# q and k transposed whole and split behind the transpose; scores as three 32-row products; interleaved tap chains

## The chip, the cores and the metric

The kernel runs on one core of a Trainium2 chip. The metric is the time of one execution on the device in microseconds (us); lower is better. The engines are called as the profile calls them: PE (TensorE; its weight loads are shown apart as PEld), DVE (VectorE), ACT (ScalarE), POOL (GpSimd) and SP, whose queue issues most DMAs.

## The reference

Two layers of a decoder trunk on 512 tokens of width 1024, in f32. The part that the change touches, cut to what matters:

```python
u = rmsnorm(h, mix_norm[i]) @ w_in[i]                 # 9 blocks of 256 columns
a_val, a_gate, pool_in, q, k, v, gb, gc, sv = split(u)
# conformer mixer: a causal depthwise convolution of 31 taps, then layer norm and silu
y = causal_dwconv(a_val * sigmoid(a_gate), conv_w) + conv_b
# differential attention: 4 heads, each with 2 q/k pairs of 32 dims, v of 64 dims
q, k = apply_rope(q), apply_rope(k)
sc = einsum("bqhcd,bkhcd->bhcqk", q, k) * 32 ** -0.5
a = softmax(where(causal, sc, -inf)); a = a[:, :, 0] - lam * a[:, :, 1]
o = rmsnorm(a @ v, subln_g) * (1 - lam_init)
h = h + concat([y_a, y_b, y_c, y_d]) @ w_out[i]
h = h + hier_moe(rmsnorm(h, ffn_norm[i]), ...)        # 16 experts, two per token
h = h + sigmoid(rmsnorm(h, ple_norm[i]) @ ple_gate_w[i] + b) * (p[i] @ ple_proj[i])
```

## The kernel before, in words

The 512 tokens are four tiles of 128. Each layer goes through five stages in order: `project` (the input projection and three of the mixers), `attend` (attention, the output projection, norms and router logits), `route`, `experts` and `combine`. Every engine takes its instructions in the order in which the program issues them, and that order is written by hand.

Products that must keep f32 accuracy are done in fp32r, a form that PE streams in one pass: each operand is split into a rounded high part and a remainder, and three products are added, high by high, high by low and low by high (`mm3`, lines 255 to 257). ACT makes the high part and DVE the remainder, for weights at L228 and L239.

`attend` is a loop of 18 ticks. Tick n starts the scores of step n (query tile n // 4, head n % 4), takes the maxima of step n - 1 (L770, DVE), its exponentials (L784, ACT) and the combination of the two softmaxes (L797, DVE), transposes the result of step n - 2 (L804, PE, evicted at L806 by ACT) and multiplies that of step n - 3 by v (L816, PE). The list `TICK` is the order within a tick, and `FILL1` and `FILL2` say how many half products of the output projection (`wo_mm`, added into h at L750 by DVE) PE does in between. What is left of the 31 taps of each half of the convolution channels waits in a queue from which `due` takes a few in each tick, as `TAPS` tells (L483, DVE), then the layer norm of that mixer. `rotate` (L632 to L635, DVE) applies the rotary tables to eight heads-and-parts of q or k of one tile.

q and k go into the scores as stacks. For a tile i and p = 0 (q) or 1 (k), `stack` lets ACT write the high part twice into `qks` (L708 the rounding, L709 the second copy) and `stack_lo` lets DVE write the remainder (L713), so that a head's 32 dims become 96: for q high, remainder, high and for k high, high, remainder. `qkt` transposes four such stacks at a time (L721, PE, 128x96 each) and evicts them (L723, ACT) into `QT` or `KT`, 96 partitions deep. One matmul of 96 rows (L762) is then the whole three-part product of one q/k pair, and a second adds the causal mask in bf16 (L763). A step has two pairs. A tile needs 4 passes of ACT of 128x256 for the stacks, 16 transposes and 4 evictions of 96x512.

Of the kernel before, what the change touches and what calls it, by code (L numbers as in the profile page):

```python
# [11 lines left out]
F32 = mybir.dt.float32  # L12
F32R = mybir.dt.float32r
# [10 lines left out]
S = 512  # L24
# [25 lines left out]
TAILU, POST, FIRST, FIRST4 = 9, 3, 5, 1  # L50
HI = {5: 1, 6: 2, 9: 3, 10: 4}

TICK = "qkt max add av out exp f1 stl turn stk due lo rot score hi f2 comb".split()
TAPS = [1.8, 2.4, 2.4, 4.8, 1.8, 1.2, 5.4, 0, 0, 0.6, 3.6, 0, 0, 1.2, 3.4, 0, 1.0, 3.4]
ROT = {0: [(2, 0)], 2: [(2, 1)], 3: [(3, 1)], 4: [(3, 0)]}
STK = {0: [(1, 1)], 2: [(2, 0)], 3: [(2, 1)], 5: [(3, 0)], 7: [(3, 1)]}
STL = {1: [(1, 1)], 3: [(2, 0)], 5: [(2, 1)], 6: [(3, 0)], 8: [(3, 1)]}
OUTD = [1, 2, 3, 4]
LND, LNT = [1, 2, 3, 4, 4, 6], [0, 1, 2, 4]
FND = [1, 1, 2, 2, 4]  # L60
# [107 lines left out]
class _Kernel:  # L168
# [262 lines left out]
    def project(self):  # L431
        nc, V, G, T, SC, w, tk = self.nc, self.V, self.G, self.T, self.SC, self.w, self.ticks
# [44 lines left out]
        def tap(m, k):  # L477
            def f():
                if k == 0:
                    V.tensor_scalar(acc[:, m], glu[:, m, 0:S], self.cwh[:, m, 0:1], self.cb[:, m:m + 1],  # L480
                                    op0=ALU.mult, op1=ALU.add)
                else:
                    V.scalar_tensor_tensor(acc[:, m], glu[:, m, k:k + S], self.cwh[:, m, k:k + 1], acc[:, m],  # L483
                                           op0=ALU.mult, op1=ALU.add)
            return f

        def ev_a():
            for m in range(2):
                V.scalar_tensor_tensor(glu[:, m, 30:], th[m], 1.0, oa[m], op0=ALU.add, op1=ALU.mult)
            for m in range(2):  # L490
                for k in range(31):
                    tk.queue.append((0.6, tap(m, k)))
            tk.queue.append((10.0, self.layer_norm))


        up = pb_.tile([128, 2, 16 + S], F32, name="up", tag="pad", bufs=1)
        G.memset(up[:, :, :16], 0.0)
        o_up = self.cm_unit(ev_a, 1.2)
        W_ = 16 + S
        sums = []  # L500
# [192 lines left out]
    def attend(self):  # L693
        V, T, SC, w, tk, sm, l = self.V, self.T, self.SC, self.w, self.ticks, self.sm, self.l
        mhi, mlo, h = self.mhi, self.mlo, self.h
        kp = self.pool("kp", side=self.side[0])
        KT = kp.tile([96, 8, S], F32R, name="KT")
        xp = self.xp
        a2 = self.pool("a2", side=self.side[1])
        QT = {}  # L700
        stk = {}


        qks = xp.tile([128, 2, 8, 3, 32], F32, name="qks", bufs=1)

        def stack(i, p):
            s_ = stk[i, p] = qks[:, p]
            SC.copy(s_[:, :, 0, :].bitcast(F32R), self.qr[i][:, 8 * p:8 * p + 8])  # L708
            SC.copy(s_[:, :, 2 - p, :], s_[:, :, 0, :])  # L709

        def stack_lo(i, p):
            s_ = stk[i, p]
            V.tensor_sub(s_[:, :, 1 + p, :].bitcast(F32R), self.qr[i][:, 8 * p:8 * p + 8], s_[:, :, 0, :])  # L713

        def qkt(i, p, b):
            s_ = stk[i, p]
            if p == 0 and b == 0:
                QT[i] = kp.tile([96, 8, 128], F32R, name="QT", bufs=2)
            pt = self.tr([128, 4, 128])
            for c in range(4):  # L720
                T.transpose(pt[:96, c], s_[:, 4 * b + c].rearrange("p a d -> p (a d)"), self.ident)  # L721
            hs = slice(4 * b, 4 * b + 4)
            SC.copy(QT[i][:, hs] if p == 0 else KT[:, hs, i * 128:(i + 1) * 128], pt[:96])  # L723

        CH = [[2, 3, 6, 7], [0, 1, 4, 5]]
        wo = {}
# [2 lines left out]
        def wo_get(kh, nh):  # L729
            wo[kh, nh] = [tuple(t.rearrange("p (c n) -> p c n", c=2) for t in w.get(0)) for _ in range(2)]  # L730
# [21 lines left out]
        st = {}  # L752

        def scores(n):
            qi, hd = divmod(n, 4)
            k = max(256, (qi + 1) * 128)
            qs_ = slice(qi * 128, (qi + 1) * 128)
            st[n] = []
            for c in range(2):
                pt = self.mm([128, 512])  # L760
                keys = KT[:, 2 * hd + c, :k] if qi else KT[:, 2 * hd + c, None, :128].to_broadcast([96, 2, 128])
                T.matmul(pt[:, :k], QT[qi][:, 2 * hd + c], keys, start=True, stop=False)  # L762
                T.matmul(pt[:, qs_], self.identb, self.maskb, start=False, stop=True)  # L763
                st[n].append(pt)

        def maxi(n):
            k = (n // 4 + 1) * 128
# [43 lines left out]
        def av(n):  # L811
            qi, hd = divmod(n, 4)
            at = st.pop(n)
            hs = slice(hd * 64, (hd + 1) * 64)
            for b in range(qi + 1):
                T.matmul(oacc[:, qi % 2, hs], at[:, b], self.vt[b][:, hs], start=(b == 0), stop=(b == qi))  # L816
# [40 lines left out]
        rr, xts, tp = {}, {}, None  # L857
# [4 lines left out]

        def fn2(i):

            p, tag = ((self.gpool, "gv0"), (xp, "qks"), (tp, "xn"), (xp, "xt"))[i]
            xx = self.scaled(i, rr[i], gffn, p, 1, "xn", tag)
            SC.dma_start(xnd[i * 128:(i + 1) * 128, :], xx)

# [26 lines left out]
        def filler(n, k):  # L895

            while k > 0 and (cur or (fill and fill[0][0] <= n)):
                if not cur:
                    a = fill.pop(0)[1]
                    cur.append((a, wo_mm(*a)))  # L900
                    next(cur[0][1])
                else:
                    (i, nh, kh), g = cur.pop()
                    next(g)
                    if (nh, kh) == (1, 1) and i < 2:
                        for d, f in zip(FND, (fn1, fn3, fn2, fn4, fn5)):
                            tk.later(d, lambda f=f, i=i: f(i))
                k -= 1

        w.limit = self.moe_start[l] + 3  # L910
        for p in range(2):
            stack(0, p)
            stack_lo(0, p)
        wo_get(0, 0)
        for p in range(2):
            for b in range(2):
                qkt(0, p, b)
        filler(0, 2)
        for p in range(2):
            self.rotate(1, p)  # L920
        wo_get(0, 1)
        stack(1, 0)
        stack_lo(1, 0)
        filler(0, 1)
        base = w.cur
        NS = 4 * NT
# [17 lines left out]
        def each(table, f):  # L944
            def g(n):
                for a in table.get(n, ()):
                    f(*a)
            return g

        steps = {  # L950
            "av": lambda n: n >= 3 and av(n - 3),
            "qkt": lambda n: n < NS - 4 and qkt(n // 4 + 1, n % 4 // 2, n % 2),
            "out": o_start,
            "add": lambda n: wo_add(),
            "max": lambda n: 1 <= n <= NS and maxi(n - 1),
            "exp": lambda n: 1 <= n <= NS and expo(n - 1),
            "turn": turns,
            "due": lambda n: tk.tick(TAPS[n]),
            "score": lambda n: n < NS and scores(n),
            "comb": lambda n: 1 <= n <= NS and comb(n - 1),  # L960
            "rot": each(ROT, self.rotate),
            "stk": each(STK, stack),
            "stl": each(STL, stack_lo),
            "lo": lambda n: w.make_lo(),
            "hi": lambda n: n in HI and w.make_hi(base + HI[n]),
            "f1": lambda n: filler(2 * n, FILL1[n]),
# [2 lines left out]
        for n in range(NS + 2):  # L969
            for a in TICK:  # L970
                steps[a](n)
# [605 lines left out]
```

## Time and profile before

| what | value |
|---|---|
| median of 3 runs | 927.7 us (925.6 to 927.95) |
| the profiled execution's own time | 925.41 us |
| its span, first to last instruction | 923.6 us |
| mean granted PE clock | 0.973 |
| busy in the span: PE, DVE, ACT | 858.0, 715.4, 519.1 us |
| `attend` of the two layers, roughly | 121 to 221 us and 572 to 673 us |

A time is in us from the start of the span. The profiled execution has 1.8 us outside of its span and is 2.3 us below the median of the runs. A matmul's row lasts from its start until its result is written, so that rows overlap: the distance from one start to the next is what a matmul costs in a stream. The same holds, less strongly, on DVE and ACT.

### The profile page before, as it was taken

Reading aid. Unit: us, or ns where it says so; the run is one execution under the profiler, and the core shown is the slowest. Engines: PE = TensorE matmul, PEld = TensorE weight load, DVE = VectorE, ACT = ScalarE, POOL = GpSimd, SP = SyncE. Lnnn points to the kernel's source line nnn. Section 1 sums busy time; section 2 is a strip of 40 time slices with the busy share of each in tenths; the row PEclk is TensorE's granted clock in tenths of the full one; section 3 lists DMA queues with packets and bytes.
Section 4 is the critical chain, followed back from the end, with each engine's and each line's share of the span. In section 5 each row is a group of like instructions: output and inputs, shape, how many; then the busy total and the mean of one; then the engine's idle time right before and its main releaser. Section 6 shows DMA issues by size and latency. Waiting matters only on the chain. (4 is left out here: it accounts for less than half of the span.)

```text
span 923.6 us, 12348 instructions
## 1 busy us (share of the span) xinstructions
PE 858.0 (93%) x4393; PEld 687.6 (74%) x4393; DVE 715.4 (77%) x1182; ACT 519.1 (56%) x945; POOL 151.2 (16%) x214
## 2 busy tenths in 40 slices
PE   7999988897999999979979999989979999998994
PEld 5888876685677777767878887767847777776783
DVE  4599989966788888746676998998478888885674
ACT  4322246853687878745433233487347778776453
POOL 2040001122222211101010300022131222111101
PEclk9999999998999999999999999989979999999998
DMA  9222230158799979563322223110958998882602
GB/s 354 106 92 96 98 114 1 46 193 309 270 347 363 370 271 340 227 234 146 114 92 92 92 103 112 49 46 24 373 216 307 359 370 324 317 321 91 260 24 91
DMA packets 35775, 179.02 MB, mean 194 GB/s; under 512 B 8064, under 2 KB 8320, under 8 KB 18944
## 3 DMA queue, kind: packets, MB, share of 16 engines
q1 hardware_dynamic: 23472, 148.49, 43.1%
q0 software_dynamic: 9792, 20.99, 6.2%
q10 hardware_dynamic: 2448, 8.73, 2.6%
q8 instruction: 35, 0.57, 0.2%
q14 instruction: 28, 0.23, 0.1%
HBM read 171.89 MB, written 23.07 MB: 211 GB/s over the span
## 5 line engine op out<-in xcount | busy, mean ns | idle before, releaser
L239 DVE TENSOR_TENSOR wl<-wr,wh 128x1024 fp32r<-128x1024 f32 x212 | 253.1, 1220 | 41.4 <-ACT wh L228 40.1
L228 ACT CAST wh<-wr 128x1024 fp32r<-128x1024 f32 x212 | 216.2, 1053 | 91.1 <-PE mm L256 60.9
L255 PE MATMUL mm<-wh,xTh 128*128 128x512 f32 x256 | 113.9, 445 | 1.0 <-ACT xTh L221 1.0
L483 DVE SCALAR_TENSOR_TENSOR acc<-glu,cwh,acc 128x512 f32<-128x512 f32 x120 | 100.5, 837 | 3.4
L257 PE MATMUL mm<-wh,xTl 128*128 128x512 f32 x256 | 101.2, 395 | 1.2 <-DVE xTl L222 1.2
L256 PE MATMUL mm<-wl,xTh 128*128 128x512 f32 x256 | 100.5, 392 | 0.0
L257 PE MATMUL mm<-nhi,wl 128*128 128x512 f32 (+1 forms) x224 | 77.3, 345 | 2.5 <-DVE wl L239 2.5
L255 PE MATMUL mm<-nhi,wh 128*128 128x512 f32 (+1 forms) x224 | 77.1, 344 | 0.0
L256 PE MATMUL mm<-nlo,wh 128*128 128x512 f32 (+1 forms) x224 | 77.0, 344 | 0.0
L255 PEld LDWEIGHTS mm<-wh,xTh 128*128 128x128 f32 x256 | 48.1, 188 | 16.9 <-issue 6.7
L1241 PE MATMUL mm<-wr,hT 128*128 128x512 f32 x128 | 60.2, 592 | 0.0
L1198 POOL DMA_INDIRECT xg<-xnd,ix x32 | 35.4, 1105 | 149.8 <-PE tr L251 136.8
L256 PEld LDWEIGHTS mm<-wl,xTh 128*128 128x128 f32 x256 | 48.2, 188 | 15.3 <-DVE wl L239 6.2
L257 PEld LDWEIGHTS mm<-wh,xTl 128*128 128x128 f32 x256 | 48.0, 188 | 12.9 <-DVE xTl L222 2.9
L255 PE MATMUL mm<-wh,mhi 128*128 128x512 f32 x128 | 54.0, 422 | 1.0 <-DVE h L750 1.0
L1203 POOL DMA_INDIRECT yd<-ys,ix x32 | 32.3, 1010 | 122.9 <-ACT ys L1243 107.3
L255 PE MATMUL mm<-wh,n3h 128*128 128x512 f32 x128 | 50.6, 395 | 0.0
L257 PE MATMUL mm<-wh,mlo 128*128 128x512 f32 x128 | 50.3, 393 | 0.0
L256 PE MATMUL mm<-wl,mhi 128*128 128x512 f32 x128 | 50.0, 391 | 0.0
L257 PE MATMUL mm<-wh,n3l 128*128 128x512 f32 x128 | 49.9, 390 | 0.0
L256 PE MATMUL mm<-wl,n3h 128*128 128x512 f32 x128 | 49.9, 390 | 0.0
L257 PEld LDWEIGHTS mm<-nhi,wl 128*128 128x128 f32 x224 | 42.4, 189 | 8.2 <-DVE wl L239 3.2
(236 smaller groups left out, 1861.6 us busy)
## 6 DMA issues: line engine op xcount, KB each, us to landing
wr<-wgu SPq DMA_DIRECT2D x62, 1024.0 KB, 9.1
wr<-wdn SPq DMA_DIRECT2D x30, 1024.0 KB, 10.8
wr<-win SPq DMA_DIRECT2D x13, 1024.0 KB, 6.2
wr<-wout SPq DMA_DIRECT2D x8, 1024.0 KB, 4.8
wr<-wpg SPq DMA_DIRECT2D x8, 1024.0 KB, 13.8
yt<-yd SPq DMA_DIRECT2D x12, 512.0 KB, 8.1
wr<-wqk SPq DMA_DIRECT2D x4, 1024.0 KB, 4.8
xnd<-xn ACTq DMA_DIRECT2D x8, 512.0 KB, 4.0
```

The source lines that it names most:

```text
L228: self.SC.copy(hi, src)
L239: self.V.tensor_sub(lo, src, h32)
L255: self.T.matmul(o, lh, rh, start=first, stop=False)
L256: self.T.matmul(o, lh, rl, start=False, stop=False)
L257: self.T.matmul(o, ll, rh, start=False, stop=last)
L483: V.scalar_tensor_tensor(acc[:, m], glu[:, m, k:k + S], self.cwh[:, m, k:k + 1], acc[:, m], op0=ALU.mult, op1=ALU.add)
L1198: return self.G.indirect_dma_start(out=dst, out_offset=None, in_=self.xnd[:, :], in_offset=bass.IndirectOffsetOnAxis(ap=col, axis=0), boun ...
L1203: return self.G.indirect_dma_start(out=self.yd[:, :], out_offset=bass.IndirectOffsetOnAxis(ap=col, axis=0), in_=src, in_offset=None, bound ...
L1241: self.T.matmul(o[nh], hT[:, c], wc[:, ns], start=(c == 0), stop=(c == 1))
```

## The change

`stack` and `stack_lo` go, and with them the tile `qks` and the two entries of `TICK` that call them. `qkt(i)` now transposes q and k of a tile as they are, four heads-and-parts of 32 dims at once (128x128), 4 transposes into one PSUM tile; ACT writes the rounded high parts of q and of k from there (two instructions of 128x256), and `qkl(i)` lets DVE write the two remainders, from PSUM too. It is called in one tick of four (`QKT = 2`) and no longer in each. `KT` and `QT` are 128 partitions deep and there is one of each for the high and for the low part; a pair's 32 dims lie in partitions r + 32c to r + 32c + 31, with r = 0 or 64 by the head. `scores` issues three products of 32 rows for each of the two pairs, the pairs in turn, and then the two masks. The taps of the two halves of the channels are queued in turn, and not all of one half before the other. `fn2(1)` writes to a tile of its own in the place of `qks`.

```diff
-        def stack(i, p):
-            s_ = stk[i, p] = qks[:, p]
-            SC.copy(s_[:, :, 0, :].bitcast(F32R), self.qr[i][:, 8 * p:8 * p + 8])
-            SC.copy(s_[:, :, 2 - p, :], s_[:, :, 0, :])
-        def stack_lo(i, p):
-            s_ = stk[i, p]
-            V.tensor_sub(s_[:, :, 1 + p, :].bitcast(F32R), self.qr[i][:, 8 * p:8 * p + 8], s_[:, :, 0, :])
-        def qkt(i, p, b):
-            s_ = stk[i, p]
-            if p == 0 and b == 0:
-                QT[i] = kp.tile([96, 8, 128], F32R, name="QT", bufs=2)
-            pt = self.tr([128, 4, 128])
-            for c in range(4):
-                T.transpose(pt[:96, c], s_[:, 4 * b + c].rearrange("p a d -> p (a d)"), self.ident)
-            hs = slice(4 * b, 4 * b + 4)
-            SC.copy(QT[i][:, hs] if p == 0 else KT[:, hs, i * 128:(i + 1) * 128], pt[:96])
+        def parts(i):
+            return QT[i], [t[:, :, i * 128:(i + 1) * 128] for t in KT]
+        def qkt(i):
+            QT[i] = [kp.tile([128, 2, 128], F32R, name=f"QT{a}", bufs=2) for a in "hl"]
+            pt = qkp[i] = self.tr([128, 2, 2, 128])
+            for p in range(2):
+                for m in range(2):
+                    T.transpose(pt[:, p, m], self.qr[i][:, 8 * p + 4 * m:8 * p + 4 * m + 4].rearrange("p a d -> p (a d)"),
+                                self.ident)
+                SC.copy(parts(i)[p][0], pt[:, p])
+        def qkl(i):
+            pt = qkp.pop(i)
+            for p, (hi, lo) in enumerate(parts(i)):
+                V.tensor_sub(lo, pt[:, p], hi.bitcast(F32))
...
+            m, r = hd // 2, 64 * (hd % 2)
+            pts = st[n] = [self.mm([128, 512]) for c in range(2)]
+            for j, (a, b) in enumerate(((0, 0), (1, 0), (0, 1))):
+                for c in range(2):
+                    rs = slice(r + 32 * c, r + 32 * c + 32)
+                    keys = KT[b][rs, m, :k] if qi else KT[b][rs, m, None, :128].to_broadcast([32, 2, 128])
+                    T.matmul(pts[c][:, :k], QT[qi][a][rs, m], keys, start=(j == 0), stop=False)
             for c in range(2):
-                pt = self.mm([128, 512])
-                keys = KT[:, 2 * hd + c, :k] if qi else KT[:, 2 * hd + c, None, :128].to_broadcast([96, 2, 128])
-                T.matmul(pt[:, :k], QT[qi][:, 2 * hd + c], keys, start=True, stop=False)
-                T.matmul(pt[:, qs_], self.identb, self.maskb, start=False, stop=True)
-                st[n].append(pt)
+                T.matmul(pts[c][:, qs_], self.identb, self.maskb, start=False, stop=True)
...
-            for m in range(2):
-                for k in range(31):
+            for k in range(31):
+                for m in range(2):
                     tk.queue.append((0.6, tap(m, k)))
...
-        for p in range(2):
-            stack(0, p)
-            stack_lo(0, p)
+        qkt(0)
         wo_get(0, 0)
-        for p in range(2):
-            for b in range(2):
-                qkt(0, p, b)
+        qkl(0)
         filler(0, 2)
         for p in range(2):
             self.rotate(1, p)
         wo_get(0, 1)
-        stack(1, 0)
-        stack_lo(1, 0)
         filler(0, 1)
```

## Rows read from the trace of the kernel before

**Rows 1.** The page's head and its busy times.
```profile
span 923.6 us, 12348 instructions
PE 858.0 (93%) x4393; PEld 687.6 (74%) x4393; DVE 715.4 (77%) x1182; ACT 519.1 (56%) x945; POOL 151.2 (16%) x214
```

**Rows 2.** Windows of `attend`: busy us per engine, PE clock, DMA share, GB/s.
```profile
122.00:170.00 48.00, 42.07 (x237) 33.41 (x237) 45.02 (x118) 32.25 (x94) 5.66 (x13) 0.97 0.19 72
170.00:178.00 8.00, 6.41 (x43) 5.15 (x42) 6.84 (x15) 7.94 (x21) 1.95 (x1) 0.95 0.00 1
178.00:220.00 42.00, 41.98 (x273) 36.41 (x273) 25.69 (x55) 22.27 (x53) 7.81 (x14) 1.00 0.56 217
573.50:621.50 48.00, 42.04 (x235) 33.39 (x236) 44.76 (x118) 31.75 (x92) 5.64 (x13) 0.96 0.19 72
621.50:630.00 8.50, 7.65 (x45) 6.24 (x43) 7.03 (x17) 8.36 (x23) 1.94 (x1) 0.81 0.01 2
630.00:672.00 42.00, 41.87 (x270) 36.25 (x270) 25.90 (x55) 22.22 (x54) 7.54 (x14) 1.00 0.62 238
```

**Rows 3.** Waits of DVE, 122.5 to 178 us: total, times, longest.
```profile
DVE fac L795 <- ACT e L784: 0.7, 1, 0.7
DVE wl L239 <- ACT wh L228: 0.6, 1, 0.6
DVE ss L833 <- ACT sq L824: 0.4, 1, 0.4
```

**Rows 4.** Timeline of DVE, first layer, start of `attend`.
```profile
122.07 0.42 DVE L713 TENSOR_TENSOR qks<-qr,qks 128x256 fp32r<-128x256 f32 x1 [2.38 <-ACT qks L708]
...
123.16 0.28 DVE L632 TENSOR_TENSOR rs<-qr,rope 128x128 f32<-128x128 f32 x1
...
126.31 2.36 DVE L239 TENSOR_TENSOR wl<-wr,wh 128x1024 fp32r<-128x1024 f32 x2 [0.56 <-ACT wh L228]
128.59 0.42 DVE L713 TENSOR_TENSOR qks<-qr,qks 128x256 fp32r<-128x256 f32 x1
128.93 0.68 DVE L750 TENSOR_TENSOR h<-h,mm 128x512 f32<-128x512 f32 x1
129.52 3.10 DVE L483 SCALAR_TENSOR_TENSOR acc<-glu,cwh,acc 128x512 f32<-128x512 f32 x4
```

**Rows 5.** Groups by line and shape: weight remainders; taps' min/median/max in ns.
```profile
L239 DVE TENSOR_TENSOR wl<-wr,wh 128x1024 fp32r<-128x1024 f32 x212 | 253.1, 1220 | 41.4 <-ACT wh L228 40.1
...
L483 DVE SCALAR_TENSOR_TENSOR acc<-glu,cwh,acc x120: 737/752/1831, 46.0 to 594.3; 128x512 f32<-128x512 f32 x120
```

**Rows 6.** Timeline of ACT, first layer, start of `attend`.
```profile
121.15 0.59 ACT L641 COPY qr<-mm 128x512 f32<-128x512 f32 x1 [2.18 <-PE mm L257]
...
125.21 2.02 ACT L228 CAST wh<-wr 128x1024 fp32r<-128x1024 f32 x2
```

**Rows 7.** Groups of ACT by line, 121 to 200 us.
```profile
L723 ACT CAST KT<-tr 96x512 fp32r<-96x512 f32 x8 | 4.6, 587 | 2.5 <-PE tr L721 2.5
...
L708 ACT CAST qks<-qr 128x256 fp32r<-128x256 f32 x8 | 3.3, 412 | 0.0
...
L822 ACT COPY on<-oacc 128x256 f32<-128x256 f32 x3 | 1.1, 377 | 0.0
```

**Rows 8.** Timeline of PE, first layer: transposes of stacks, a step of scores, streams.
```profile
122.64 1.93 PE L721 MATMUL tr<-con,qks 128*96 128x128 f32 x16 [1.59 <-DVE qks L713]
...
182.20 0.48 PE L762 MATMUL mm<-KT,QT 96*128 96x512 f32 x1
...
182.56 0.47 PE L762 MATMUL mm<-KT,QT 96*128 96x512 f32 x1
...
182.94 0.83 PE L816 MATMUL oacc<-v,at 128*128 128x64 f32 x6
...
183.90 0.39 PE L256 MATMUL mm<-wl,mhi 128*128 128x512 f32 x1
184.13 0.40 PE L257 MATMUL mm<-wh,mlo 128*128 128x512 f32 x1
...
188.27 1.86 PE L883 MATMUL mm<-par,xt 128*128 128x20 f32 x16
```

More of the change, by code (lines that the diff above doesn't have):

```diff
@@ L51 @@
 HI = {5: 1, 6: 2, 9: 3, 10: 4}
-TICK = "qkt max add av out exp f1 stl turn stk due lo rot score hi f2 comb".split()
+TICK = "qkt max add av out exp f1 qkl turn due lo rot score hi f2 comb".split()
 TAPS = [1.8, 2.4, 2.4, 4.8, 1.8, 1.2, 5.4, 0, 0, 0.6, 3.6, 0, 0, 1.2, 3.4, 0, 1.0, 3.4]
 ROT = {0: [(2, 0)], 2: [(2, 1)], 3: [(3, 1)], 4: [(3, 0)]}
-STK = {0: [(1, 1)], 2: [(2, 0)], 3: [(2, 1)], 5: [(3, 0)], 7: [(3, 1)]}
-STL = {1: [(1, 1)], 3: [(2, 0)], 5: [(2, 1)], 6: [(3, 0)], 8: [(3, 1)]}
+QKT = 2
 OUTD = [1, 2, 3, 4]
@@ L696, in attend @@
         kp = self.pool("kp", side=self.side[0])
-        KT = kp.tile([96, 8, S], F32R, name="KT")
+        KT = [kp.tile([128, 2, S], F32R, name=f"KT{a}") for a in "hl"]
         xp = self.xp
         a2 = self.pool("a2", side=self.side[1])
-        QT = {}
-        stk = {}
-        qks = xp.tile([128, 2, 8, 3, 32], F32, name="qks", bufs=1)
-        def stack(i, p):
-            s_ = stk[i, p] = qks[:, p]
-            SC.copy(s_[:, :, 0, :].bitcast(F32R), self.qr[i][:, 8 * p:8 * p + 8])
-            SC.copy(s_[:, :, 2 - p, :], s_[:, :, 0, :])
-        def stack_lo(i, p):
-            s_ = stk[i, p]
-            V.tensor_sub(s_[:, :, 1 + p, :].bitcast(F32R), self.qr[i][:, 8 * p:8 * p + 8], s_[:, :, 0, :])
-        def qkt(i, p, b):
-            s_ = stk[i, p]
-            if p == 0 and b == 0:
-                QT[i] = kp.tile([96, 8, 128], F32R, name="QT", bufs=2)
-            pt = self.tr([128, 4, 128])
-            for c in range(4):
-                T.transpose(pt[:96, c], s_[:, 4 * b + c].rearrange("p a d -> p (a d)"), self.ident)
-            hs = slice(4 * b, 4 * b + 4)
-            SC.copy(QT[i][:, hs] if p == 0 else KT[:, hs, i * 128:(i + 1) * 128], pt[:96])
+        QT, qkp = {}, {}
+        def parts(i):
[12 more added lines that the diff above has]
+                V.tensor_sub(lo, pt[:, p], hi.bitcast(F32))
         CH = [[2, 3, 6, 7], [0, 1, 4, 5]]
@@ L757, in scores @@
             qs_ = slice(qi * 128, (qi + 1) * 128)
-            st[n] = []
-            for c in range(2):
-                pt = self.mm([128, 512])
-                keys = KT[:, 2 * hd + c, :k] if qi else KT[:, 2 * hd + c, None, :128].to_broadcast([96, 2, 128])
-                T.matmul(pt[:, :k], QT[qi][:, 2 * hd + c], keys, start=True, stop=False)
-                T.matmul(pt[:, qs_], self.identb, self.maskb, start=False, stop=True)
-                st[n].append(pt)
+            m, r = hd // 2, 64 * (hd % 2)
[5 more added lines that the diff above has]
+                    T.matmul(pts[c][:, :k], QT[qi][a][rs, m], keys, start=(j == 0), stop=False)
+            for c in range(2):
+                T.matmul(pts[c][:, qs_], self.identb, self.maskb, start=False, stop=True)
         def maxi(n):
@@ L863, in fn2 @@
         def fn2(i):
-            p, tag = ((self.gpool, "gv0"), (xp, "qks"), (tp, "xn"), (xp, "xt"))[i]
+            p, tag = ((self.gpool, "gv0"), (xp, "xn"), (tp, "xn"), (xp, "xt"))[i]
             xx = self.scaled(i, rr[i], gffn, p, 1, "xn", tag)
@@ L951, in attend @@
             "av": lambda n: n >= 3 and av(n - 3),
-            "qkt": lambda n: n < NS - 4 and qkt(n // 4 + 1, n % 4 // 2, n % 2),
+            "qkt": lambda n: n < NS - 4 and n % 4 == QKT and qkt(n // 4 + 1),
+            "qkl": lambda n: n < NS - 4 and n % 4 == QKT and qkl(n // 4 + 1),
             "out": o_start,
@@ L961, in attend @@
             "rot": each(ROT, self.rotate),
-            "stk": each(STK, stack),
-            "stl": each(STL, stack_lo),
             "lo": lambda n: w.make_lo(),
```

## The prediction, made before the changed kernel ran

> **What bounds the kernel now.** I read the page first: PE is busy for 93% of the span, DVE for 77%, ACT for 56% [rows 1]. That average hides the stage that is changed, so I cut `attend` of both layers into three windows each. In the first 48 us of the loop DVE is the fullest engine, 45.02 of 48 us, with PE at 42.07 and ACT at 32.25; in the 8 us that follow ACT has 7.94 of 8; in the last 42 PE has 41.98, DVE 25.69 [rows 2]. The second layer repeats it. So one stage has three limits in turn, and a saving counts only on the engine whose turn it is. The waits of DVE confirm the first: in 55 us it waits for other engines in three places of any size, 0.6, 0.7 and 0.4 us [rows 3]. In its timeline it goes from one instruction to the next from 122.07 us on [rows 4]. [...]
>
> **The change on ACT.** A tile costs four evictions at 0.587 us (8 rows of KT in a layer, and as many of QT at the same length) and four passes for stacks at 0.412 (L708; L709 is alike) [rows 7]: 4.0 us. After it are two copies of 128x256 out of PSUM; the nearest row is L822, 0.377 us: 0.75 us. ACT is relieved of 3.2 us a tile, 13 us a layer. Nearly all of it lies where ACT has slack and is worth nothing there. It counts in two places, below.
>
> **The change on DVE, first window.** The remainder (L713, 128x256) is replaced by one of the same size read from PSUM; between a gain and a loss of 0.1 us I take nothing, eight for eight. What moves is the start.
>
> - Before: DVE stands idle for 2.38 us until ACT has made the first high part, and starts the rotation of tile 1 at 123.16 [rows 4]. After: ACT is free at 121.15 + 0.59 = 121.74 [rows 6], copies twice 0.37, and the second remainder can start at 122.5; PE's four transposes are done before that if their PSUM banks are free, since its last projection is over. DVE issues the next instruction some 0.34 us after a remainder (128.59 to 128.93), so the rotation starts at 122.83, 0.33 us earlier.
> - ACT's two weight casts stood at 125.21, behind stacks and evictions [rows 6]; they can now start near 122.5, so the wait of 0.56 us at L239 [rows 4] goes. Together 0.89.
> - The remainder at 128.59 leaves this place (0.34 earlier), but six must be made in the loop in place of five (0.34 later): nothing.
> - Taps: four in a row take 3.10 us [rows 4] at 0.752 each [rows 5], so they start 0.783 apart: each needs the one before, which writes the same accumulator. Two remainders of weights, which don't need each other, take 2.36 at 1.220 each: the second starts 0.08 before the first ends. Interleaved, neighbours belong to different accumulators, so I expect 0.752 - 0.08 = 0.67 from start to start, 0.11 less. Three such groups lie in the loop with three distances each: 9 x 0.11 = 1.0 us. The other 50 taps of a layer run in `project` under a PE that is full there, and I count them at nothing. If PE had slack there, they would be worth 5.5 us a layer; if the distance were not the dependence, the whole is 0.
>
> Sum of the first window: 1.9 us a layer.
>
> **Second window.** DVE waits 0.7 us for exponentials and 0.4 for squares, both from an ACT that is full [rows 2, 3]. One tile's 3.2 us off ACT covers these. 1.1 us, between 0 and, if PE's waits were all that counted, 1.6 (the two windows' idle of PE is 8.00 - 6.41 there).
>
> **PE.** Sixteen transposes take (1.93 - 0.27) / 15 = 0.11 us each [rows 8]; twelve of sixteen go, 1.3 us a tile, 5.3 us a layer. All of it lies in the first two windows, where PE is not the limit: it pays for the longer scores there and, beyond, is worth nothing. If DVE weren't in the way it would be worth those 5.3.
>
> The scores count in the third window, where the last four steps lie, 512 keys each, and PE is full. A step costs 182.94 - 182.20 = 0.74 us, its first half 182.56 - 182.20 = 0.36: 0.23 for the product (the stream distance, 184.13 - 183.90) and 0.13 for the mask and the change between number forms [rows 8]. I split that, as an estimate, into 0.05 for a mask and 0.09 for a change. After: six products, two masks, one change, 0.19 beside the products. No row of before has a 32-row product, so the price lies between two ends:
>
> - one after another, as everything in the stream goes: 6 x 0.23 + 0.19 = 1.55, 0.81 more, 3.2 us a layer;
> - the two pairs at the same time: 3 x 0.23 + 0.19 = 0.87, 0.13 more, 0.5 us a layer. Six loads don't forbid that: sixteen small matmuls with a load each start (1.86 - 0.27) / 15 = 0.11 apart [rows 8], 0.66 for six.
>
> I take the lower end. The two products of a pair use different rows of the array and different PSUM tiles, and PE takes up a matmul 0.23 us after one that lasts 0.39, so it doesn't wait for ends. It is a choice and not a reading.
>
> Between 96-row and 128-row products the trace shows no wait beyond those 0.09 us [rows 8]. [...]
>
> **SP and buffers.** `KT` and `QT` take less room, and the ring that opens when their pool closes issues its loads at the same tick. These move with the stage.
>
> **Sum.** 1.9 + 1.1 - 0.5 = 2.5 us a layer, 5 us for two. What follows each stage (routing, experts, a PE that is full) starts earlier by that. From the profiled 925.4 us that makes 920.4; as that execution lies 2.3 below the median of 927.7, I forecast 922.6 for the median. A difference of 0.3%, 2.8 us, is about what a measurement of this kernel can tell from none.
>
> **Rivals.**
>
> 1. *The products go one after another* (upper end): 3.0 - 3.2 a layer, 0.5 us slower, 928.2. For it: the stream shows nothing else. Chance 0.15.
> 2. *Each change of row group waits until the product before has ended* (the other side). Then a product costs its 0.39 us, a step 6 x 0.39 + 0.10 = 2.44, 1.7 more, 6.8 us a layer against 3.0 gained: 7.6 us slower, 935. It decides once a step costs more than 0.74 + 3.0 / 4 = 1.5 us. Against it: matmuls here start before the last one ends. Chance 0.12.
> 3. *Only going into the 32-row form and out of it drains*: twice 0.39 - 0.23 = 0.16 a step, 1.3 us a layer, 925.3. [...] Chance 0.10.
> 4. *A new wait on DVE.* `qkl` stands behind ACT's copies, these behind PE's transposes at the head of the tick; all that DVE has in the tick (taps, rotations, the combination) is queued behind it, and PE's transposes wait for the combination. If DVE comes early each time, it waits for four transposes and one copy, 3 x 0.11 + 0.38 = 0.7 us, at three ticks, 2.1 us a layer: 926.8. Against it: DVE comes late to what others give it in that window [rows 3]. Chance 0.08.
> 5. *The clock stays up.* The first two windows lost 0.03 x 48 + 0.05 x 8 = 1.8 us of full-rate PE time in the first layer and 0.04 x 48 + 0.19 x 8.5 = 3.5 in the second [rows 2]. If a PE with fewer waits keeps the upper level and all of that counts, 5.3 us more: 917.3. Against it: DVE holds PE back there all the same. Chance 0.09.
>
> **Numbers.** The forecast has 0.46, with its own range from 919.5 (PE's waits all gone) to 925 (the taps worth nothing and 0.4 a layer less elsewhere). Faster by over 0.3% are the forecast and rival 5: 0.55. Within 0.3%: rivals 3 and 4 and most of 1 (0.12): 0.30. Slower: rival 2 and the rest of 1 (0.03): 0.15. The range from 916 to 930 leaves out rival 2.
>
> **What would show it.** In the profile of the changed kernel: the first rotation of `attend` near 122.8, no wait of L239 for its cast there; taps 0.67 apart; ACT at under 7 of 8 us before the last window; pairs of score products that start within a few hundredths of a us, a step of some 0.87 us at 512 keys; PE still full to the end of the stage, which ends 2.5 us earlier in each layer. I am wrong if the products of a pair start 0.23 or more apart, if DVE shows a wait of its own at the new remainders, or if another engine holds what DVE gains before PE's window begins.

## The result and the profile after

The changed kernel takes 937.73 us in the median of 4 runs (936.38 to 940.7), the kernel before 927.02 us beside it: a ratio of 1.0121, 95% interval 1.0090 to 1.0152. It is slower by 1.2%, where 922.6 us and a gain were forecast. The profiled execution is the one of 936.38 us, 10.97 above the profiled one of before.

The line numbers of the changed kernel are one or a few lower: `mm3` is L254 to L256, the new transposes are L711, ACT's two copies L713, DVE's remainders L718, the scores L760, the masks L762.

The page, as in [rows 1]:

```profile
span 934.5 us, 12343 instructions
PE 867.2 (93%) x4425; PEld 687.5 (74%) x4425; DVE 708.0 (76%) x1182; ACT 497.5 (53%) x897; POOL 152.2 (16%) x214
```

DVE and ACT did become lighter, by 7.4 and 21.6 us. PE is busy for 9.2 us more. The windows of `attend`, as in [rows 2] (length, busy time of PE, PEld, DVE, ACT and POOL with their instructions, granted clock, DMA share, GB/s):

```profile
122.00:170.00 48.00, 40.91 (x222) 29.80 (x223) 41.47 (x111) 20.95 (x67) 5.65 (x13) 0.93 0.18 63
170.00:178.00 8.00, 7.54 (x38) 5.59 (x37) 7.05 (x19) 6.35 (x18) 1.27 (x1) 0.50 0.20 85
178.00:228.00 50.00, 49.17 (x318) 41.68 (x317) 30.66 (x64) 26.79 (x61) 8.22 (x16) 0.97 0.45 177
573.50:621.50 48.00, 40.78 (x228) 30.03 (x226) 39.94 (x106) 19.62 (x62) 4.52 (x9) 1.00 0.17 58
621.50:642.00 20.50, 19.53 (x81) 14.78 (x82) 15.62 (x41) 13.57 (x39) 3.08 (x5) 0.51 0.11 46
642.00:684.00 42.00, 41.98 (x281) 35.75 (x281) 22.73 (x45) 20.76 (x46) 5.79 (x14) 1.00 0.63 239
```

Two things are to be seen. No engine is full in the first window any more: DVE has 41.47 of 48 us and PE 40.91, so they wait for one another (the rows of waits below). And the clock column: all of 170 to 178 us is at the lower level (0.50; the clock's records of this execution hold two levels, 1.00 and 0.50), and in the second layer nearly all of 20.5 us (0.51). There PE is busy for 19.53 of 20.5 us, at half speed: it has become the limit by its clock. The clock's records give the stretches at the lower level between the start of the loop and its last four steps: before 3.4 and 6.8 us in the two layers, after 17.1 and 20.5.

The waits of PE, 122 to 178 us (who waits for whom, us in total, times, longest), then that of DVE at the new remainders, then the longest wait of PE in the same window of the kernel before:

```profile
PE tr L711 <- ACT QTh L713: 2.2, 4, 0.8
PE tr L802 <- DVE e L795: 1.7, 2, 1.2
PE mm L254 <- ACT e L782: 1.5, 1, 1.5
```

```profile
DVE QTl L718 <- ACT KTh L713: 6.6, 3, 5.1
```

```profile
PE tr L721 <- DVE qks L713: 2.0, 2, 1.6
```

Two places of PE's timeline after the change, the head of the loop and step 13, one with 512 keys:

```profile
121.06 0.38 PE L711 MATMUL tr<-con,qr 128*128 128x128 f32 x2
122.22 0.44 PE L711 MATMUL tr<-con,qr 128*128 128x128 f32 x2 [0.79 <-ACT QTh L713]
...
190.01 1.27 PE L875 MATMUL tr<-con,h 128*128 128x128 f32 x8
191.22 0.50 PE L760 MATMUL mm<-KTh,QTh 32*128 32x512 f32 x2
191.55 0.39 PE L760 MATMUL mm<-KTh,QTl 32*128 32x512 f32 x2
191.78 0.40 PE L760 MATMUL mm<-KTl,QTh 32*128 32x512 f32 x2
192.11 0.28 PE L762 MATMUL mm<-maskb,identb 128*128 128x128 bf16 x2
192.23 0.83 PE L814 MATMUL oacc<-v,at 128*128 128x64 f32 x6
```

The first line of waits is new: before, PE's transposes waited for DVE's remainders (2.0 us), now they wait for ACT. q's and k's transposes lie in one PSUM tile with ACT's copy of q issued between them, and k's two wait until that copy has been made: 1.16 us from pair to pair at the head, where four transposes in a stream cost 4 x 0.11 = 0.44 together [rows 8]. The wait is handed on to DVE. Of its 6.6 us at the new remainders 5.1 are the idle time at the head, where it stood idle for 2.38 us before [rows 4]; the other 1.5 us lie in the loop, in a place where DVE had no wait before.

The step: each x2 is a pair of products, whose starts in the trace are 3 to 4 ns apart (up to 20 in other steps), so they run at the same time. (In 4 of the 32 steps of the two layers the second product starts 0.35 to 0.46 us after the first.) But a step is not 0.87 us long: 191.22 to 192.23 is 1.01. The first pair takes 0.33 to the next, the second 0.23, the third again 0.33 to the mask. And ahead of the step the eight transposes (L875) take 1.21 us. The same place in the timeline of the kernel before has 1.03:

```profile
185.38 1.27 PE L877 MATMUL tr<-con,h 128*128 128x128 f32 x8
186.41 0.48 PE L762 MATMUL mm<-KT,QT 96*128 96x512 f32 x1
```

The 0.18 stand behind the last transpose: from its start to the first product it is 0.20 us, before it was 0.03, and alike at steps 12 and 15 (at step 14 it is 0.20 for 0.11). A step at 512 keys costs 1.01 + 0.18 in place of the 0.74 of [rows 8], 0.45 more.

DVE at the start of `attend`, as in [rows 4], and ACT, as in [rows 6]:

```profile
123.10 0.42 DVE L718 TENSOR_TENSOR QTl<-tr,QTh 128x256 fp32r<-128x256 f32 x1 [5.11 <-ACT KTh L713]
123.44 0.41 DVE L718 TENSOR_TENSOR KTl<-tr,KTh 128x256 fp32r<-128x256 f32 x1
123.77 0.28 DVE L631 TENSOR_TENSOR rs<-qr,rope 128x128 f32<-128x128 f32 x1
...
126.30 2.35 DVE L238 TENSOR_TENSOR wl<-wr,wh 128x1024 fp32r<-128x1024 f32 x2
128.57 0.68 DVE L745 TENSOR_TENSOR h<-h,mm 128x512 f32<-128x512 f32 x1
129.16 2.73 DVE L482 SCALAR_TENSOR_TENSOR acc<-glu,cwh,acc 128x512 f32<-128x512 f32 x4
```

```profile
121.79 0.38 ACT L713 CAST QTh<-tr 128x256 fp32r<-128x256 f32 x1
122.70 0.37 ACT L713 CAST KTh<-tr 128x256 fp32r<-128x256 f32 x1 [0.53 <-PE tr L711]
122.97 2.00 ACT L227 CAST wh<-wr 128x1024 fp32r<-128x1024 f32 x2
```

The rotation starts at 123.77 and not 122.83: both remainders wait for ACT's copy of k, that for k's transposes, those for the copy of q. The casts stand at 122.97, DVE's wait for them is gone, and four taps take 2.73 us in place of 3.10.

### The profile page after: what moved, and what is told of

Its sections match the earlier page's. It is cut to its first block, busy times and chain, and to the rows that moved or that the text cites. A ratio compares the mean times of both kernels' runs of the same rounds, so it can differ in the third digit from the quotient of the medians.

```text
span 934.5 us, 12343 instructions
## 1 busy us (share of the span) xinstructions
PE 867.2 (93%) x4425; PEld 687.5 (74%) x4425; DVE 708.0 (76%) x1182; ACT 497.5 (53%) x897; POOL 152.2 (16%) x214
## 5 line engine op out<-in xcount | busy, mean ns | idle before, releaser
L254 PE MATMUL mm<-wh,xTh 128*128 128x512 f32 x256 | 113.9, 445 | 1.0 <-ACT xTh L220 1.0
L256 PE MATMUL mm<-wh,xTl 128*128 128x512 f32 x256 | 101.2, 395 | 1.2 <-DVE xTl L221 1.2
L482 DVE SCALAR_TENSOR_TENSOR acc<-glu,cwh,acc 128x512 f32<-128x512 f32 x120 | 90.4, 817 | 0.1
L256 PE MATMUL mm<-nhi,wl 128*128 128x512 f32 (+1 forms) x224 | 77.3, 345 | 2.6 <-DVE wl L238 2.6
L254 PE MATMUL mm<-nhi,wh 128*128 128x512 f32 (+1 forms) x224 | 77.1, 344 | 0.0
L254 PEld LDWEIGHTS mm<-wh,xTh 128*128 128x128 f32 x256 | 48.1, 188 | 16.8 <-issue 6.7
L254 PE MATMUL mm<-wh,mhi 128*128 128x512 f32 x128 | 56.0, 437 | 3.7 <-ACT e L782 3.0
L782 ACT ACTIVATE e<-mm,mx 128x128 f32<-128x128 f32 (+3 forms) x64 | 33.0, 521 | 48.1 <-DVE mx L768 48.0
L256 PEld LDWEIGHTS mm<-wh,xTl 128*128 128x128 f32 x256 | 48.0, 188 | 13.0 <-DVE xTl L221 2.9
L256 PE MATMUL mm<-wh,mlo 128*128 128x512 f32 x128 | 51.9, 406 | 0.0
L254 PE MATMUL mm<-wh,n3h 128*128 128x512 f32 x128 | 50.5, 395 | 0.0
L256 PE MATMUL mm<-wh,n3l 128*128 128x512 f32 x128 | 49.9, 390 | 0.0
```

Of the source, the lines that this page charges most:

```text
L254: self.T.matmul(o, lh, rh, start=first, stop=False)
L256: self.T.matmul(o, ll, rh, start=False, stop=last)
L782: SC.activation(ee[:, :k], pts[c][:, :k], AF.Exp, bias=mx[:, c:c + 1], accum_out=sums[qi][:, c, hd:hd + 1])
```

## The experiments

Two theories stood first. A: PE has less to do in the first two windows, the clock falls there and PE runs late. B: the new waits and the price of the 32-row form account for the loss. To compare kernels by place, this table gives the time from the start of ACT's last copy out of `project` (L641, 121.15 in [rows 6]) to the last mask of step 4, of step 12 and of step 15 and to the last router product on PE, first and second layer, from each profiled timeline; and the stretches at the lower clock that lie between step 0 and step 15:

| kernel | step 4 | step 12 | step 15 | end | lower clock |
|---|---|---|---|---|---|
| before | 28.48, 28.47 | 61.73, 62.41 | 72.99, 73.67 | 99.90, 101.34 | 3.4; 6.8 |
| after | 29.22, 27.66 | 66.21, 67.67 | 78.69, 80.16 | 105.61, 107.09 | 17.1; 20.5 |
| e1_taps | 27.44, 27.44 | 60.70, 61.64 | 71.94, 74.49 | 98.88, 101.65 | 3.4; 6.8 |
| e2_four_first | 26.83, 26.81 | 63.17, 63.35 | 75.65, 75.82 | 102.58, 102.72 | 13.7; 13.7 |
| e6_dummy_late | 26.81, 26.82 | 60.16, 60.18 | 72.65, 72.65 | 99.58, 99.58 | none |
| e8_taps_again | 27.40, 27.40 | 61.59, 60.44 | 74.44, 71.68 | 101.74, 98.61 | 6.8; none |
| e12_few_tr | 27.19, 27.57 | 59.62, 62.50 | 70.88, 73.76 | 98.00, 100.68 | 6.8; 13.7 |

**The taps alone (e1_taps)**, on the kernel before:

```diff
-            for m in range(2):
-                for k in range(31):
+            for k in range(31):
+                for m in range(2):
```

> The kernel before with one part of the change alone: the taps of the two channel halves in turn. Theory A (the loss is PE's clock, which falls because PE has less to do while DVE holds it back) and theory B (the loss is waits: k's transposes behind ACT's copy of q, the scores' price) both expect the 1.0 us a layer that the prediction counted on DVE: 2 us faster than before, 925 us, taps 0.67 us from start to start, and a clock as before. A rival, that the tap order itself unsettles the stage, expects the same time as before or a slower one, and a longer stretch at the lower clock than the 3.4 and 6.8 us of before.

923.34 us (10 runs) beside 926.37: ratio 0.9975 (0.9948 to 1.0001). By step 4 it is 1.04 and 1.03 us ahead of before in the two layers. The taps are worth what was forecast for them in `attend`; that the whole kernel gains is not clear from these runs, whose interval touches no change.

**The four transposes ahead of both copies (e2_four_first):**

```diff
                     T.transpose(pt[:, p, m], self.qr[i][:, 8 * p + 4 * m:8 * p + 4 * m + 4].rearrange("p a d -> p (a d)"),
                                 self.ident)
+            for p in range(2):
                 SC.copy(parts(i)[p][0], pt[:, p])
```

> The changed kernel with all four transposes of a tile ahead of ACT's two copies, so that k's transposes no longer wait for the copy of q. Theory B: the wait of 0.8 us at the head and of 0.46 us three times a layer goes, and with it 2 to 2.5 us a layer: 932 to 934 us. Theory A: PE stands idle elsewhere instead, since DVE sets the pace there; the stretches at the lower clock stay (17 us in the first layer, 20 in the second): 936 to 938 us.

933.45 us (5 runs), 1.0076 (1.0042 to 1.0109), as theory B has it. The order with the wait costs 4.3 us in the medians, and all five runs (930.68 to 935.62) lie under the four of the changed kernel. Step 12 comes 3.0 and 4.3 us earlier than in the changed kernel, with shorter stretches at the lower clock, so part of this is clock. What the wait costs without the clock can be read up to step 4 of the second layer, where neither kernel has left the upper level: 27.66 to 26.81, 0.85 us.

**Unread transposes (e3_dummy)**, four in each of nine ticks of the changed kernel:

```diff
+        def idle_tr():
+            pt = self.tr([128, 4, 128])
+            for c in range(4):
+                T.transpose(pt[:, c], self.ident, self.ident)
```

> The changed kernel with four transposes of the identity matrix into a spare PSUM tile, whose result nobody reads, in each of the nine ticks of a layer that had transposes of stacks before and have none now: PE's work of before is put back, the waits stay. Theory A: the clock stays at its upper level in most of the stage, the stretches at the lower level shrink from 37 us in both layers to 10 or less, and the time falls to 928 to 931 us although PE does more. Theory B: the clock has nothing to do with it; 36 more groups of 0.44 us, hidden in PE's idle time or not: 938 to 945 us.

936.33 us (4 runs), 1.0117 (1.0073 to 1.0161), between the ranges of the two theories: not the gain of A, nor the loss of B. In the first layer the clock stayed up until the last router product, and step 12 came at 62.68 in place of 66.21; in the second, with the waits still in place, 17 us at the lower clock remained and step 15 came at 82.04 in place of 80.16.

**The pairs issued one after the other (e4_serial):** all three products of one row group, then all three of the other.

```diff
-            for j, (a, b) in enumerate(((0, 0), (1, 0), (0, 1))):
-                for c in range(2):
+            for c in range(2):
+                for j, (a, b) in enumerate(((0, 0), (1, 0), (0, 1))):
```

> The changed kernel with the three products of one pair issued before the three of the other, so that neighbours use the same row group. The prediction's choice of pairs at the same time (which the changed kernel's trace shows) expects six starts 0.23 us apart at 512 keys in place of three pairs, 0.65 us more a step there. Theory B: 3 us a layer more, 943 to 945 us. Theory A: PE is busy for longer in the stretch that loses its clock; if that holds the clock up, it gives back up to 6 us a layer, and the time is 934 to 940 us.

936.89 us (6 runs), 1.0108 (1.0073 to 1.0142), as the changed kernel. It lies in the range of theory A, but not for its reason: the order did not matter. The timeline of PE at a step shows why:

```profile
189.57 0.51 PE L760 MATMUL mm<-KTh,QTh 32*128 32x512 f32 x2
189.91 0.40 PE L760 MATMUL mm<-KTh,QTl 32*128 32x512 f32 x2
190.15 0.39 PE L760 MATMUL mm<-KTl,QTh 32*128 32x512 f32 x2
190.47 0.28 PE L762 MATMUL mm<-maskb,identb 128*128 128x128 bf16 x2
```

Issued as three and three, they still run as three pairs. That the order of issue did change is seen at the start of a step: the first weight loads of the two groups are 10 ns apart in 28 of the 32 steps, where they are 3 to 4 ns apart in the changed kernel. So PE starts the first product of the second group 0.33 us before the second product of the first group, which the program issues ahead of it: between row groups, PE doesn't keep to the order of the program. The experiment therefore says nothing of what one-after-another products would cost; it says that two row groups go on independently.

**The masks between the products (e5_mask_between)**, on e2_four_first: four changes of form in a step in place of two.

```diff
-                    T.matmul(pts[c][:, :k], QT[qi][a][rs, m], keys, start=(j == 0), stop=False)
+                    T.matmul(pts[c][:, :k], QT[qi][a][rs, m], keys, start=(j == 0), stop=(j == 2))
+                if j == 0:
+                    for c in range(2):
+                        T.matmul(pts[c][:, qs_], self.identb, self.maskb, start=False, stop=False)
-            for c in range(2):
-                T.matmul(pts[c][:, qs_], self.identb, self.maskb, start=False, stop=True)
```

> The changed kernel with the four transposes first (933.45), and the two masks of a step moved from its end to behind the first pair of products: the same eight matmuls, but four changes between 32-row and full-height work in a step and not two. Theory B (a change costs, about 0.18 us going in and 0.10 coming out): a step at 512 keys lasts 0.28 us longer, the distance from step 12 to step 15 grows from 12.47 by 3 x 0.28 = 0.8 us, and the kernel by between 2.2 us (only the eight steps under a full PE count) and 5 us: 935.7 to 938.5. Rival (a change is free, and the 32-row products themselves last longer than 0.23): the distance stays at 12.5 and the time at 933.5.

941.29 us (4 runs), 1.0162 (1.0132 to 1.0193), 7.8 above its own base and more than the 938.5 that theory B allows. Its timeline at a step with 512 keys:

```profile
190.25 0.50 PE L761 MATMUL mm<-KTh,QTh 32*128 32x512 f32 x2
190.69 0.29 PE L764 MATMUL mm<-maskb,identb 128*128 128x128 bf16 x2
190.91 0.50 PE L761 MATMUL mm<-KTh,QTl 32*128 32x512 f32 x2
191.24 0.40 PE L761 MATMUL mm<-KTl,QTh 32*128 32x512 f32 x2
191.57 0.88 PE L816 MATMUL oacc<-v,at 128*128 128x64 f32 x6
```

1.32 us in place of 1.01 for the same eight matmuls: two more changes cost 0.31, 0.28 was expected. So it is the change of form that costs, not the length of a 32-row product. The rest of the 7.8 us isn't taken apart: a stretch of 3.4 us at the lower clock fell also on the last steps of either layer, and from step 12 to step 15 it is 15.07 us in place of 12.48.

**The clock, with the waits mended (e6_dummy_late):** e2_four_first, with `idle_tr` as above in the ticks 5, 7, 8, 9 and 11.

> The changed kernel with the four transposes first (933.45), and four transposes of the identity, which nobody reads, in each of the ticks 5, 7, 8, 9 and 11 (20 x 0.11 = 2.2 us of PE work a layer, just ahead of and in the place where its clock fell for 13.7 us in each layer). Theory A (what is left of the loss beside the scores is the clock, and it falls because PE has less to do there): the stretches in attend shrink to the 3.4 and 6.8 us of before or vanish, and the time falls by 3 to 7 us, to 926 to 930. Rival (the clock falls where PE would wait anyway and costs nothing): 933 to 936, whether the stretches vanish or not.

926.27 us (10 runs) beside 925.34: ratio 1.0008 (0.9985 to 1.0031). 2.2 us of added work in a layer made the kernel 7.2 us faster by the medians, and 6.3 by the two ratios, each taken beside its own runs of before. The windows 170 to 178 and 619 to 639 us of e2_four_first and then of e6_dummy_late, with the columns of the windows above:

```profile
170.00:178.00 8.00, 8.00 (x36) 6.62 (x35) 7.57 (x19) 7.21 (x19) 1.94 (x1) 0.50 0.00 0
619.00:639.00 20.00, 19.98 (x101) 15.38 (x102) 15.71 (x41) 13.89 (x38) 3.08 (x5) 0.66 0.08 32
```

```profile
170.00:178.00 8.00, 6.84 (x45) 4.96 (x44) 7.78 (x18) 7.18 (x19) 1.94 (x1) 1.00 0.02 6
619.00:639.00 20.00, 18.83 (x129) 14.50 (x129) 17.99 (x44) 15.45 (x42) 3.06 (x5) 1.00 0.00 1
```

Clock 0.50 and PE full with 36 matmuls; clock 1.00 and PE with room left over 45. Up to step 4 the two kernels agree within 0.02 us; at step 12 the clock is worth 3.0 and 3.2 us a layer. The mean granted clock of a whole execution, which is on record for every run and not for the profiled one alone, says the same: 0.958 to 0.966 in the 5 runs of e2_four_first (0.963 in the median), 0.976 in the median of these 10. One of the 10 lies at 0.960 and takes 932.16 us, so the unread work lowers the chance of a fall and doesn't rule it out. In a stream without gaps, products of 512 columns start 0.43 us apart at a granted clock of 0.50 and 0.23 at 1.00 (changed kernel, L254 to L256, 179.34 to 180.19 and 182.71 to 183.63 us). As an estimate from these, 13.7 us under a PE that is full throughout would cost 13.7 x (1 - 0.23 / 0.43) = 6.4. The trace shows half of it, 3.0 to 3.2. PE had room in that place: from 165 to 170 us it is busy for 4.53 of 5 us even at the lower clock (e2_four_first), and at the upper one for 6.84 of 8 us from 170 to 178 (e6_dummy_late).

**Real work moved later (e7_refill):** e2_four_first, with the half projections that fill PE's gaps spread later: of sixteen, the last five lie in ticks 7, 8 and 9, where two lay in tick 7 (the expectation counts six).

```diff
-FILL1 = [0, 1, 1, 1, 1, 1, 0, 5, 1, 1, 1, 1, 1, 4, 0, 1, 0, 2, 1, 1, 0, 0, 0, 0, 0, 0, 0, 0, 0]
-FILL2 = [4, 0, 1, 0, 0, 1, 0, 4, 1, 0, 0, 1, 0, 0, 0, 1, 2, 1, 2, 1, 2, 2, 4, 2, 2, 2, 0, 0, 0]
+FILL1 = [0, 1, 1, 1, 1, 1, 0, 1, 1, 1, 1, 1, 1, 4, 0, 1, 0, 2, 1, 1, 0, 0, 0, 0, 0, 0, 0, 0, 0]
+FILL2 = [2, 0, 0, 0, 0, 1, 0, 1, 1, 1, 0, 1, 0, 0, 0, 1, 2, 1, 2, 1, 2, 2, 4, 2, 2, 2, 0, 0, 0]
```

> The changed kernel with the four transposes first (933.45), and real work in place of unread transposes: of the sixteen half projections that fill PE's gaps, seven are done later, so that the last six lie in ticks 7, 8 and 9 in place of two in tick 7 alone. Theory A: PE stays busier where the clock fell, the stretches of 13.7 us shrink, and the time falls by 3 to 7 us to 926 to 930 with no added work. Rival (they are wanted early, because PE has room there, and are in PE's way later): 935 or more.

937.36 us (4 runs), 1.0139 (1.0107 to 1.0171): a miss. The clock stayed up at 165 us, but in the first layer fell for 10.2 us at 144.5, behind the ticks from which the work was taken, for 3.4 at 178.7 and for 6.8 at 195.7, under the last steps. In the second it fell three times for 3.4 us up to step 12.

**The taps again, and with unread transposes (e8_taps_again, e9_taps_dummy).** The second is e1_taps with `idle_tr` in the ticks 7, 9 and 11.

> The kernel before with the tap chains interleaved and nothing else, once more and in more rounds, because its interval of 0.9948 to 1.0001 just touched no change. All theories: 923.5 to 924.5, 2 to 3 us under before, with an interval that ends below 1.

> The kernel before with interleaved taps (923.3 and 924.1), and four unread transposes in the ticks 7, 9 and 11: its attend still has 3 to 7 us at the lower clock in a layer. If that costs as it did in the changed kernel (half of the stretch where PE is full), they vanish and the time is 921 to 923. Rival (the unread work costs what the clock gives, 12 x 0.11 = 1.3 us a layer): 924 to 926.

924.08 us (12 runs), ratio 0.9986 (0.9965 to 1.0006), where an interval below 1 was expected, and 924.46 us (12 runs), 0.9983 (0.9966 to 0.9999). Three sets of runs with interleaved taps lie 0.14 to 0.25% below before, two of the intervals just touch no change: the taps are the part to keep, and a small gain. The unread transposes add nothing there: a stretch of 3.4 us remained in either layer.

**Unread work in 32 rows (e10_dummy_32row):** as e6_dummy_late, with another kind of unread work.

```diff
-            for c in range(4):
-                T.transpose(pt[:, c], self.ident, self.ident)
+            for j in range(4):
+                for c in range(2):
+                    rs = slice(32 * c, 32 * c + 32)
+                    T.matmul(pt[c][:, :256], QT[n // 4][0][rs, 0], KT[0][rs, 0, :256], start=(j == 0), stop=(j == 3))
```

> The kernel with the four transposes first and unread work in the ticks 5, 7, 8, 9 and 11 (926.3, no stretch at the lower clock between 122 and 210 us), with the unread work in another form: in place of four full-height transposes (4 x 0.11 us) four pairs of 32-row products with 256 columns (4 x about 0.12 us, and a change of form ahead of and behind them). Theory A1 (what counts is that PE does something): the clock stays up in attend, and the time is 926 to 930. Theory A2 (work in 32 rows does not hold the clock, and the scores in that form are a cause of the stretches): the stretches of 10 us and more come back, and the time is 932 or more.

936.06 us (4 runs), 1.0092 (1.0063 to 1.0122), as A2 has it, 9.8 above e6_dummy_late. Stretches of 10.2 us stand at 147.3 and 178.0 us in the first layer; in the second there are only two of 3.4. It doesn't prove A2: the first begins ahead of the first unread product, and the products take two of the three PSUM tiles for transposes at once, for one of which PE waits:

```profile
161.92 0.38 PE L948 MATMUL tr<-KTh,QTh 32*128 32x256 f32 x1
162.53 0.73 PE L948 MATMUL tr<-KTh,QTh 32*128 32x256 f32 x7 [0.23 <-ACT acc L672]
```

**The unread transposes without the mended wait (e11_after_dummy):** the changed kernel with `idle_tr` in the ticks 5, 7, 8, 9 and 11.

> The changed kernel as it is (k's transposes behind ACT's copy of q, 937.7), with the same unread transposes in the ticks 5, 7, 8, 9 and 11. If the two losses add up (waits 4 us, clock 7 us): the clock stays up in attend and the time is 930 to 931. Rival (with the waits in it the clock falls anyway, because they leave PE idle): stretches of 10 us and more stay, and the time is 934 or more. Second rival (the waits cost only through the clock): 926 to 927.

937.06 us (4 runs), 1.0097 (1.0062 to 1.0132). The two losses don't add up: with the wait in place the clock falls anyway (10.2 us in the first layer up to step 12, 3.4 in the second, and 6.8 us under the last steps of either). In the first layer PE stood still for 1.49 us behind ACT's copy of q, until 172.88, and the clock fell at 174.4:

```profile
172.88 0.44 PE L711 MATMUL tr<-con,qr 128*128 128x128 f32 x2 [1.49 <-ACT QTh L713]
```

In the changed kernel that wait was 0.79 us at most.

**Fewer transposes with the old scores (e12_few_tr)**, on e1_taps:

```diff
-            for c in range(4):
-                T.transpose(pt[:96, c], s_[:, 4 * b + c].rearrange("p a d -> p (a d)"), self.ident)
+            T.transpose(pt[:96, 0], s_[:, 4 * b].rearrange("p a d -> p (a d)"), self.ident)
-            SC.copy(QT[i][:, hs] if p == 0 else KT[:, hs, i * 128:(i + 1) * 128], pt[:96])
+            SC.copy(QT[i][:, hs] if p == 0 else KT[:, hs, i * 128:(i + 1) * 128],
+                    pt[:96, 0, None, :].to_broadcast([96, 4, 128]))
```

> The kernel before with interleaved taps (923.3 to 924.5), where only one of each four transposes of q and k is made and its block is copied to all four places (it leaves out three quarters of the transposes, and its scores are not those of the reference). PE has the same 12 transposes a tile less to do as in the changed kernel, the scores keep their 96-row form, and the evictions, the stacks and the waits stay. Theory A1 (the clock fell in the changed kernel because PE had less to do): stretches of 10 us and more appear in attend, and the time is 928 or more. Theory A2 (the 32-row form of the scores, or the waits, are needed for that): stretches as in the kernel with interleaved taps, 3 to 7 us a layer, and 921 to 924.5.

923.13 us (10 runs) beside 925.97: ratio 0.9971 (0.9952 to 0.9989). Half of each theory: the stretches grew to 6.8 and 13.7 us, as A1 has it for the second layer, but the time did not, as A2 has it. The granted clock of all runs confirms that it falls: 0.962 to 0.972 here, 0.966 in the median, against 0.966 to 0.981, 0.975, in the 22 runs of e1_taps and e8_taps_again, while before had a median of 0.973 beside each of them. What the clock took, the transposes left out gave back: at step 12 it is 1.1 us ahead of e1_taps in one layer and 0.9 behind in the other.

## Why the prediction was wrong

Per layer, by the table and at the end of the stage, the changed kernel lost 5.7 us (105.61 - 99.90, and 107.09 - 101.34) where 2.5 were to be gained. From after to e2_four_first it is 3.0 and 4.4 (the wait, and the clock that goes with it), from there to e6_dummy_late 3.0 and 3.1 (the clock alone), and e6_dummy_late is 0.3 and 1.8 ahead of before.

- **First window, 1.9 forecast: nearly right, once the wait is mended.** 1.65 at step 4 (28.48 to 26.83), of which the taps are 1.03 to 1.08 (forecast 1.0) and the earlier start some 0.6 (forecast 0.89). In the changed kernel itself the start was late by 0.94 us (123.77 for 122.83).
- **The step that failed first: "PE's four transposes are done before that if their PSUM banks are free".** They were costed as one group of four. In the program ACT's copy stands between the second and the third, in the same PSUM tile, and PE waits for it each time, with all that is queued on PE behind it. The fourth rival had a wait of this chain, on DVE, at 2.1 us a layer. It came there, at 1.5 us in the loop of the first layer, and on PE as well, at 2.2. The whole step is worth 4.3 us of the kernel's time (e2_four_first), a part of it by the clock. What a write of PE beside ACT's read of the same tile would do is not shown, as no run here lets the two meet; the order from which the wait comes (0.79 us at the head) stands in the diff.
- **The step that failed most: the twelve transposes that go were "worth nothing" where PE isn't the limit, and the clock of before was kept in the sum.** The fifth rival let it only rise. It fell, and took 3 us a layer after the wait was mended. PE's slack was not free: with twelve transposes a tile fewer the granted clock falls from 0.975 to 0.966 in the median of the runs (e12_few_tr), and with twenty unread ones a layer put back it rises from 0.963 to 0.976 (e2_four_first to e6_dummy_late).
- **The third window, 0.5 forecast, mis-sized.** From step 12 to step 15 it is 12.48 us for 11.26, 0.41 a step, 1.6 for four. That the pairs run at the same time, the choice on which the term hung, was right (3 to 4 ns apart), and rival 1 and rival 2 are out. The change of form was costed at 0.09; going in costs 0.18 + 0.10 and coming out 0.10. A price for going in and coming out is what the third rival had, put at 2 x 0.16 = 0.32 a step above the forecast; measured is 0.41 - 0.13 = 0.28, and two more changes in a step cost 0.31 us (e5_mask_between). The runs show the price; that PE drains at a change was the author's assumption and is not shown.
- **Second window, 1.1 forecast: not seen.** ACT did fall to 6.35 of 8 us (7.18 with the clock up, e6_dummy_late). But from step 4 to step 12 e6_dummy_late takes 33.35 us, and e8_taps_again in the layer with the clock up 33.04, with ACT's work as before. Part of that is the scores, which are longer there too; the rest isn't taken apart.
- With the waits and the clock mended, what is gained ahead of the last steps and the price of the scores cancel: 1.0008. No version run here that keeps the reference's scores gave more than the taps alone.

**What stays open:** which property of the work lets the clock fall. Less work for PE lowers the clock by itself (0.975 to 0.966 in the median, e12_few_tr), a standing PE seems to (1.49 us, and the fall 1.5 us later, e11_after_dummy), and 32-row work didn't stand in for full-height work (two stretches of 10.2 us where e6_dummy_late has none, e10_dummy_32row, which is mixed with a wait). The stretches at the lower clock differ between the layers of one kernel and between executions of the same kernel (e1_taps and e8_taps_again), so one profile of each doesn't decide it. How the 4.3 us of the mended order divide between the wait and the clock is open beyond the 0.85 us up to step 4. That the lower clock costs about 3 us a layer here is shown by e6_dummy_late; what set it off is not.

## What to carry to other kernels

A saving on PE "off the critical path" is to be looked at twice where a full stretch follows: list what PE has left to do there, and price the case that its clock falls (here 13.7 us at the lower clock cost 3.0 to 3.2). When an instruction group is fused into one PSUM tile, write down the issue order, and ask at each write whether a reader of the same tile stands ahead of it; here one line moved was worth 4.3 us. Two 32-row products run side by side in the time of one (at 512 keys 3 to 4 ns apart, with the next pair 0.23 us after them inside the form), but going into that form and out of it has a price, here 0.18 + 0.10 + 0.10 us, and it counts once for each step that lies between full-height work.

## What the runs showed of the hardware

- The two row groups take their products independently of the order of issue, and PE starts a product ahead of one of the other group that was issued before it: issued as three and three, the products of a pair start 3 to 10 ns apart in the step shown (e4_serial), where they start 3 to 4 ns apart when issued in turn.
- PE can be at half its clock and look full: 7.54 of 8 us busy at a granted clock of 0.50 in the changed kernel, 8.00 of 8 in e2_four_first. The column of busy time alone would have shown an engine at its limit; with the clock beside it, it shows one at half speed, which in e6_dummy_late did more in 6.84 us.
- Into the 32-row form and out of it costs PE 0.17 to 0.18 us behind transposes (0.20 in place of 0.03 from the last of them to the first product), 0.10 between the first two pairs and 0.10 ahead of the masks; two more changes in a step cost 0.31 (e5_mask_between).
- A product of 512 columns in fp32r starts 0.23 us after the one before it in a stream [rows 8]; in plain f32 it is 0.43 (L1241 of the kernel before: four in a row from 251.17 us take 1.88, the last of them 0.59). The number of passes behind that is not shown.
- Work whose result nobody reads can pay for itself: twenty transposes a layer, 2.2 us, took the kernel from 933.45 to 926.27 us in the medians, with the clock up in `attend` of the profiled execution (e6_dummy_late).
